# Fetching three 2 MB weight matrices in eighths between attention steps instead of whole ahead of them (hybrid decoder trunk, eight cores)

## The chip, the cores and the metric

The kernel runs on all 8 cores of one Trainium2 chip. Each core works on one prompt sequence of 2048 tokens and 16 single-token samples; the cores exchange nothing. The metric is the device time of the slowest core in microseconds. An execution is marked *slow* when one die (four cores) takes over 1% longer than the other at a lower granted TensorE clock, or when it is over 1.5% above the fastest of the same kernel; all others are *fast*, and slow runs are not compared with fast ones. Ratios below are the record's, of fast runs against fast runs of the same rounds, so they are not quite the ratio of the medians quoted.

## The reference

Two layers, each `x += mixer(norm(x)); x += memory_attention(norm(x)); x += mlp(norm(x))`, for a prompt group and a sample group that share all weights. What matters here is the attention of one layer and the MLP that follows it:

```python
def mem_attend(u, k, v, w_q, w_o):            # 4 heads of 256, 256 memory rows
    q = einsum('btd,de->bte', u, w_q)
    s = einsum('bthd,bnhd->bhtn', q, k) * (MEM_HEAD_DIM ** -0.5)
    p = softmax(s)
    return einsum('btd,de->bte', einsum('bhtn,bnhd->bthd', p, v), w_o)

def sq_relu_mlp(u, w_up, w_down):             # D_FF = 4096, done in four quarters
    h = relu(einsum('btd,df->btf', u, w_up))
    return einsum('btf,fd->btd', h * h, w_down)
```

Every sample has its own cached K and V (1 MB each in f32). Every prompt core has one K and V for its whole sequence, already multiplied into the weights.

## The kernel before

Weights live in five slots of SBUF, each one 1024 x 1024 matrix in bf16 (2 MB, for which 4 MB of f32 are read). `load` takes a free slot and starts one DMA from GpSimd (POOL), which casts f32 to bf16 on the way:

```python
def load(name, at=None):
    t = claim(name, at)
    dma(POOL, t(), DV(wsrc_sq(wsrc[name])), f"w{slot_of[name]}")
```

Just before the attention of a layer, the kernel loads the first quarter's up and down matrices and the second quarter's up matrix (`up0_0`, `dn0_0`, `up0_1`), each as soon as its slot is free. The MLP that needs them comes more than 100 us later.

During the attention, TensorE walks five tiles of the prompt. Twice per tile a *sample step* is put in between:

```python
def SDV(b):                                    # load V of sample b, in two halves
    v = VS[b % 2]
    for x in range(2):
        memset(v(x, sl(0, 4), sl(256, 257)), 1.0, eng=POOL)
        dma(POOL, v(x, sl(0, 4), sl(0, 256)), DV(cv_d[l, b, x*128:(x+1)*128, :]...), f"v{nm}{b % 2}")

def SA(b):                                     # scores of sample b on TensorE and DVE
    ...
    memset(PBZ[b % 2](), 0.0, eng=POOL)        # "the clear": empties the probability tile

def SE(b):                                     # ScalarE: probabilities into the tile
    act(PBZ[b % 2](sl(0, 8), b), SS(b % 4), AF.Exp, scale=1.0 / 16.0)

def sample(b):                                 # one sample step
    if b % N_ATT_S:
        SB(b - 1)                              # TensorE: PBZ times V, the "sample product"
    if b < last:
        SDK(b + 1); SDV(b + 1)
    SA(b)
```

`SE(b-1)` is called two chunks of matmuls before `sample(b)`; where nothing was late it started some 1.9 us before the sample product (249.68 and 251.55 us in the kernel before). GpSimd therefore runs, in this order and step after step: V half 0 of the next sample, V half 1, the clear. ScalarE's `SE` waits for the clear, and TensorE's sample product waits for `SE`.

A tracker derives every wait. Two of its lines matter:

```python
# Tracker.access: who must be waited for
if s.w is not None:
    deps.add(s.w)                              # the last writer of these bytes
if write:
    deps.update(s.rc.values())                 # and their readers
# Prog.add: how a DMA is waited for
if d.kind == "d":
    dw[d.chan] = self.chan_count[d.chan] * 16  # ALL DMAs issued so far on its semaphore
```

A DMA is waited for by the *current* count of its semaphore, not by its own. That is cautious for a good reason: the Trainium skill, "DMA: Bandwidth & Descriptors", section "Why a DMA increments its semaphore by 16 and not by 1", says that when two DMAs in flight share one semaphore, a lower count can be reached before the earlier one has fully landed.

The softmax here doesn't subtract the row's maximum and nothing guards it: scores larger than these inputs give would overflow.

## Time and profile before

| | before |
|---|---|
| median time, fast | 1732.6 us (1731.6 to 1734.0, 4 runs) |
| TensorE busy | 1599.2 us, 93% of the span |
| stall before the first sample product, layer 0 | 10.44 us |
| stall before the second sample product, layer 1 | 5.38 us |

From the page of the kernel before: the span, and TensorE's busy time, share and instructions.

```profile
span 1728.7 us, 28840 instructions; the slowest of 8 cores (1719.0 to 1728.7 us)
PE 1599.2 (93%) x9989; PEld 912.1 (53%) x10000; DVE 889.0 (51%) x1928; ACT 569.1 (33%) x1054; POOL 99.8 (6%) x218
```

TensorE is the bound. What can be won is its idle time. (PE is TensorE, PEld its weight loads, DVE VectorE, ACT ScalarE, POOL GpSimd. L350 is the helper through which every DMA is issued, L347 that of memsets, L315 that of ScalarE's activations; so instructions are told apart by their tiles.) The timeline of GpSimd around the start of layer 0's attention (start and duration in us; in brackets, the idle time before and what ended it):

```profile
161.19 1.08 POOL L350 DMA_DIRECT2D MEM<-w_up  x1 [30.86 <-PE PS L291]
183.09 0.87 POOL L350 DMA_DIRECT2D MEM<-w_down  x1 [20.82 <-PE PS L291]
186.64 0.87 POOL L350 DMA_DIRECT2D MEM<-w_up  x1 [2.68 <-PE PS L291]
...
187.58 0.75 POOL L350 DMA_DIRECT2D MEM<-cv  x1
...
222.97 0.74 POOL L350 DMA_DIRECT2D MEM<-cv  x1 [0.40 <-issue]
...
227.21 0.74 POOL L350 DMA_DIRECT2D MEM<-cv  x1 [3.37 <-DMA MEM<-cv]
```

Three matrices are issued just ahead of the first V load (`cv`), and the V load behind them took 33.4 us to land, by the chain of waits, where the median of all `cv` loads of that core is 5.0. The last two lines show something else: the second half of a V load goes out 4.24 us after the first, because GpSimd waits for the first to land, that is for its DMA to complete. That is the tracker's rule at work: the buffer was last written by an older DMA on the same semaphore, so half 1 waits for the count that includes half 0.

The timeline of TensorE, the two sample products (L295) that were late:

```profile
221.88 0.61 PE L295 MATMUL PS<-MEM 128*16 128x257 bf16 x8 [10.44 <-DMA MEM<-cv]
...
1126.54 0.61 PE L295 MATMUL PS<-MEM 128*16 128x257 bf16 x8 [5.38 <-ACT MEM L315]
```

The table of stretches (window, its length, busy time and instructions of five engines, granted clock, DMA share, GB/s) right after the first stall:

```profile
222.00:226.00 4.00, 4.00 (x18) 1.31 (x11) 2.30 (x11) 0.00 (x0) 0.98 (x3) 0.50 0.52 67
226.00:230.00 4.00, 3.77 (x16) 1.71 (x15) 1.04 (x6) 1.67 (x4) 0.95 (x2) 0.75 0.57 180
230.00:235.00 5.00, 5.00 (x39) 2.85 (x36) 3.66 (x7) 4.21 (x5) 0.00 (x0) 1.00 0.61 122
```

The granted clock is 0.50 for 4 us and 0.75 in the mean of the next 4, so it is halved for about 6 us after the stall. So a stall costs more than its idle time.

### The profile page before, as it was taken

The page shows a single profiled execution, that of the slowest core. Times are in us where ns is not written, and L with a number is a line of the kernel's source. Part 1 is how long each engine was busy: PE and PEld are TensorE (multiplying, and loading weights), DVE is VectorE, ACT ScalarE, POOL GpSimd, SP SyncE. Part 2 cuts the span into 40 slices and gives each one's busy share as a digit, 9 for nine tenths or more (in the row PEclk, how much of TensorE's full clock was granted, in tenths as well). Part 3 has the DMA queues.
Part 4 walks back from the last instruction along what each step waited for, and adds up shares of the span by engine and source line. Part 5 has one row for each costly group of instructions (what it writes and reads, how often), then busy time and mean ns, then how long its engine had stood idle before and what let it go on. Part 6 is the DMA issues. An engine that isn't in the chain of part 4 may idle for free.

```text
span 1728.7 us, 28840 instructions; the slowest of 8 cores (1719.0 to 1728.7 us)
## 1 busy us (share of the span) xinstructions
PE 1599.2 (93%) x9989; PEld 912.1 (53%) x10000; DVE 889.0 (51%) x1928; ACT 569.1 (33%) x1054; POOL 99.8 (6%) x218
## 2 busy tenths in 40 slices
PE   2657889999999999999999999999999999999985
PEld 2544445555565556555555555445555555555553
DVE  3544656646444444444666666666555444442357
ACT  2443633363212222223222223442552111113442
POOL 0200111011000000000000000110110000000000
PEclk9877989999999999999999999999999999999998
DMA  5959955354550740525300007954566353000112
GB/s 129 194 129 216 191 100 115 74 124 97 98 109 15 137 96 1 97 50 87 66 1 1 1 1 124 201 105 109 95 138 101 59 98 61 1 1 1 41 64 93
DMA packets 85495, 147.97 MB, mean 86 GB/s; under 512 B 3932, under 2 KB 37852, under 8 KB 85338
## 3 DMA queue, kind: packets, MB, share of 16 engines
q0 software_dynamic: 67552, 84.34, 31.6%
q1 hardware_dynamic: 17802, 61.80, 10.6%
q8 instruction: 83, 1.36, 0.3%
q14 instruction: 58, 0.48, 0.1%
HBM read 217.08 MB, written 14.36 MB: 134 GB/s over the span
## 4 chain that ended last, share of the span: by engine, by line
PE 83%; DMA 7%; DVE 5%; issue 2%; ACT 2%; SPq 0%; DVEq 0%; POOL 0%; ACTq 0%; POOLq 0%
PE PS L291 81%; DMA MEM<-cv 3%; DVE MEM L323 2%; DMA MEM<-x 2%; ACT MEM L315 2%; DVE MEM L344 2%; PE PS L295 1%; DMA MEM<-w_pool 1%; PE PS L300 1%; DMA MEM<-xs 0%; SPq L350 0%; DVE MEM L327 0%; DMA MEM<-mem 0%; DVE MEM L303 0%; ACT MEM L339 0%
## 5 line engine op out<-in xcount | busy, mean ns | idle before, releaser
L291 PE MATMUL PS<-MEM 128*128 128x416 bf16 (+6 forms) x9141 | 1530.9, 328 | 81.9 <-DVE MEM L323 64.9
L291 PEld LDWEIGHTS PS<-MEM 128*128 128x128 bf16 (+1 forms) x9152 | 849.9, 98 | 753.7 <-issue 134.7
L315 ACT ACTIVATE MEM<-PS 128x416 f32<-128x416 f32 (+6 forms) x510 | 260.2, 515 | 669.5 <-PE PS L291 605.7
L327 DVE TENSOR_TENSOR MEM<-PS,MEM 128x416 f32<-128x416 f32 (+5 forms) x525 | 295.7, 580 | 264.8 <-PE PS L291 256.0
L323 DVE SCALAR_TENSOR_TENSOR MEM<-MEM 128x416 bf16<-128x416 f32 (+8 forms) x346 | 200.3, 630 | 154.4 <-ACT MEM L315 126.4
L315 ACT ACTIVATE MEM<-MEM 128x416 bf16<-128x416 f32 (+13 forms) x317 | 204.9, 657 | 215.2 <-DVE MEM L327 106.3
L327 DVE TENSOR_TENSOR MEM<-MEM 128x416 bf16<-128x416 f32 (+4 forms) x284 | 161.8, 588 | 212.1 <-ACT MEM L315 183.8
L303 DVE SCALAR_TENSOR_TENSOR MEM<-MEM,PS 128x256 f32<-128x256 f32 x256 | 105.1, 420 | 81.0 <-PE PS L291 57.5
L339 ACT COPY MEM<-PS 128x512 f32<-128x512 f32 (+3 forms) x75 | 40.3, 538 | 118.4 <-PE PS L291 109.0
L344 DVE TENSOR_REDUCE MEM<-MEM 128x1 f32<-128x1024 f32 (+2 forms) x37 | 44.9, 1213 | 65.2 <-ACT MEM L315 65.1
L295 PE MATMUL PS<-MEM 128*16 128x257 bf16 (+2 forms) x640 | 52.0, 275 | 17.7 <-DMA MEM<-cv 10.4
L339 ACT CAST MEM<-PS 128x512 bf16<-128x512 f32 (+3 forms) x81 | 43.0, 558 | 70.4 <-PE PS L291 70.3
L295 PEld LDWEIGHTS PS<-MEM 128*16 128x16 bf16 (+2 forms) x640 | 40.2, 113 | 29.3 <-issue 28.8
L350 POOL DMA_DIRECT2D MEM<-cv x64 | 47.4, 741 | 118.8 <-DMA MEM<-cv 86.1
L315 ACT ACTIVATE PS<-PS 128x416 f32<-128x416 f32 (+3 forms) x68 | 33.4, 492 | 54.8 <-PE PS L291 54.4
L300 PE MATMUL PS<-MEM 128*128 128x128 f32 (+6 forms) x208 | 27.0, 282 | 17.6 <-DVE MEM L323 9.8
L323 DVE SCALAR_TENSOR_TENSOR MEM<-PS,MEM 128x512 f32<-128x512 f32 (+2 forms) x40 | 28.1, 743 | 15.2 <-ACT MEM L315 15.2
L300 PEld LDWEIGHTS PS<-MEM 128*128 128x128 f32 (+6 forms) x208 | 23.1, 142 | 21.2 <-issue 20.0
L347 POOL MEMSET MEM<- 128x4 bf16 (+1 forms) x96 | 14.9, 159 | 278.6 <-PE PS L295 220.8
L341 DVE CAST MEM<-PS 128x512 bf16<-128x512 f32 (+1 forms) x44 | 27.4, 640 | 5.2 <-PE PS L291 5.0
L303 DVE DVE_READ_ACCUMULATOR MEM<-MEM,PS 128x1 f32 x256 | 21.1, 82 | 0.0
L350 POOL DMA_DIRECT2D MEM<-w_down x8 | 7.0, 873 | 236.7 <-PE PS L291 224.5
(20 smaller groups left out, 78.0 us busy)
## 6 DMA issues: line engine op xcount, KB each, us to landing
MEM<-ck SPq DMA_DIRECT2D x64, 512.0 KB, 5.1
MEM<-w_up POOLq DMA_DIRECT2D x8, 2048.0 KB, 15.1
MEM<-w_down POOLq DMA_DIRECT2D x8, 2048.0 KB, 17.2
MEM<-cv POOLq DMA_DIRECT2D x64, 256.0 KB, 5.0
MEM<-x SPq DMA_DIRECT2D x16, 512.0 KB, 10.2
MEM<-w_o POOLq DMA_DIRECT2D x4, 2048.0 KB, 19.1
y<-MEM SPq DMA_DIRECT2D x15, 512.0 KB, 2.7
MEM<-w_conv_in POOLq DMA_DIRECT2D x3, 2048.0 KB, 13.4
```

Source lines behind the costliest of these rows:

```text
L291: P.add(PE, "c", lambda e, o=out.ap, l=lhsT.ap, r=rhs.ap: e.matmul(out=o, lhsT=l, rhs=r, start=start, stop=stop), [lhsT, rhs], [out])
L295: P.add(PE, "c", lambda e, o=out.ap, l=lhsT.ap, r=rhs.ap: e.matmul(out=o, lhsT=l, rhs=r, start=start, stop=stop, is_transpose=is_transpose ...
L300: P.add(PE, "c", lambda e, o=out.ap, i=in_.ap, d=ident.ap: e.transpose(out=o, in_=i, identity=d), [in_, ident], [out])
L303: P.add(DVE, "c", lambda e, o=out.ap, a=in0.ap, b=in1.ap, c=acc.ap: e.scalar_tensor_tensor(out=o, in0=a, scalar=1.0, in1=b, op0=ALU.mult, ...
L315: P.add(ACT, "c", lambda e, o=out.ap, i=in_.ap: e.activation(out=o, in_=i, func=func, bias=bias, scale=sc), rd, [out])
L323: P.add(eng, "c", lambda e, o=out.ap, a=in0.ap, b=in1.ap: e.scalar_tensor_tensor(out=o, in0=a, scalar=sc, in1=b, op0=op0, op1=op1), rd, [out])
L327: P.add(eng, "c", lambda e, o=out.ap, a=in0.ap, b=in1.ap: e.tensor_tensor(out=o, in0=a, in1=b, op=op), [in0, in1], [out])
L339: P.add(ACT, "c", lambda e, o=out.ap, i=in_.ap: e.copy(out=o, in_=i), [in_], [out])
L341: P.add(eng, "c", lambda e, o=out.ap, i=in_.ap: e.tensor_copy(out=o, in_=i), [in_], [out])
L344: P.add(eng, "c", lambda e, o=out.ap, i=in_.ap: e.tensor_reduce(out=o, in_=i, axis=AX.X, op=ALU.add), [in_], [out])
L347: P.add(eng, "c", lambda e, o=out.ap: e.memset(o, val), [], [out])
L350: return P.add(q, "d", lambda e, o=out.ap, i=in_.ap: e.dma_start(out=o, in_=i), [in_], [out], chan=chan, after=after)
```

## The change

The intent: keep the weights out of the way of the first V loads, and spread their bytes over attention tiles 1 to 3, since nobody needs them before the MLP. The diff, with the places of the calls cut to their core:

```diff
+    pieces = []
+    def load_slowly(name):
+        pieces.extend((name, kc) for kc in range(NCH))       # 8 pieces
+    def trickle():
+        if pieces:
+            name, kc = pieces.pop(0)
+            if kc == 0:
+                claim(name)
+            dma(POOL, W(name)(kc), DV(wsrc_sq(wsrc[name])[:, kc, :]), f"w{slot_of[name]}")
...
-        load(next(after))                # up0_0, dn0_0; likewise up{l}_1, up1_0, dn1_0
+        load_slowly(next(after))
...
             def mid_s(m, k=k):
+                if m % 2 and k:
+                    trickle()
...
-                O(k - 1, lambda ec: (pre() if ec == 1 else step() if ec == 3 else None))
+                O(k - 1, lambda ec: (trickle() if ec % 2 == 0 else pre() if ec == 1 else step() if ec == 3 else None))
...
-        assert not todo
+        assert not todo and not pieces
```

A piece is 128 rows of a matrix, 512 KB read and 256 KB written. Between two sample steps there are alternately three and five places for a piece. No matmul changes.

## The prediction

> **What bounds the kernel now.** TensorE: the page gives it 93% of the 1728.7 us span, and the chain of waits puts 83% on it. Idle TensorE at the ends (first 170 us, last 115 us) is untouched by this change. Two stalls are its target. The waits of layer 0's attention show TensorE idle for 10.4 us, to 221.9 us, for the first sample's V load: the timeline of GpSimd shows that load issued at 188, straight behind three whole weight matrices (161, 183, 187 us), and the chain gives the V load 33 us instead of the usual 4.5. In layer 1 a V load issued at 1104.9 lands at 1125 behind three matrices (1068 to 1086); TensorE idles 5.4 us. The Trainium skill, "TensorE: Matmul & The Clock Gate", Part 1, says an idle window of some 3.4 us halves the clock; here the granted clock is 0.89 to 0.93 around both stalls and 1.00 later, and the next sample interval takes 12.9 us instead of 10.5, so each stall costs some 2.4 us more. At stake: 10.4 + 5.4 + 2 x 2.4 = about 20 us (1.2%).
>
> **What the change does.** 3 matrices per layer become 24 pieces of 512 KB (read side), spread over attention tiles 1 to 3: no piece ahead of the first V loads, so both stalls should go. No matmul changes.
>
> **What it adds.** The kernel's dependency tracker makes a DMA that overwrites an older DMA's data wait for that channel's *current* count, including the pieces just issued. So each piece waits on GpSimd until the piece before it has landed. The trace shows this rule at work today: the second half of each V load starts 4.2 to 5.4 us after the first half (DMA wait 3.3 to 4.4 us), with a free queue. In layer 0 all three slots were last filled by a DMA, so all 24 pieces are serialized; in layer 1 two of three (the conv scratch slot was last written mostly by compute).
>
> GpSimd order per sample: V half 0, wait, V half 1, clear the small probability tile, then 3 or 5 pieces. Sample intervals on TensorE alternate 10.5 and 17.1 us (three and five pieces). Estimate, from V half 4.6 us, piece 4.0 to 4.2 us, issue 0.5 to 0.7: three pieces cost GpSimd 15 us, five cost 23; 38 per pair of samples against 27.6. The lag grows some 8 to 10 us per tile. Its victim: the clear of the probability tile comes after the second V issue, ScalarE's exponential waits for it, TensorE for that. By hand this gives layer 0 about 18 us of new stall including a re-throttle, layer 1 about 9.
>
> **Sum:** -20.7 + 18 + 10 = +7 us. Predicted 1740 us, range 1726 to 1764. Each 0.4 us on a piece moves it by about 8 to 10 us. Faster by over 2%: 0.01; within 2%: 0.92; slower by over 2%: 0.07.
>
> **What would show it.** Right: stalls at about 211 to 222 and 1121 us gone; GpSimd shows pieces spaced about 4 us with waits named DMA; V loads issued well after the sample product that frees their buffer; new TensorE idle of some 5 to 10 us twice in tiles 1 to 3 of layer 0, ended by ScalarE (behind GpSimd's memset), fewer in layer 1; clock dips there; GpSimd waiting on w_up/w_down DMAs for tens of us in total. MLP stages unchanged. Wrong: pieces issued back to back at 0.5 us (no serialization), then about 1713 us; or pieces landing in 3.4 us, then about 1727; or 5 us, about 1760.
>
> **What would make it wrong.** Piece landing time under eight cores' load; ScalarE order hiding more of the lag than I count; a slot order in layer 1 that serializes the third matrix too.

## The result, and the profile after

The change made the kernel slower: 1779.5 us median (1774.7 to 1781.7, 4 fast runs) against 1732.6, ratio 1.0266 with a 95% interval of 1.0244 to 1.0289. From the page of the kernel after:

```profile
span 1772.9 us, 28937 instructions; the slowest of 8 cores (1760.5 to 1772.9 us)
PE 1612.0 (91%) x10000; PEld 916.0 (52%) x10000; DVE 890.0 (50%) x1928; ACT 570.7 (32%) x1054; POOL 120.1 (7%) x260
```

The timeline of GpSimd in layer 0, part of tiles 1 and 2:

```profile
231.63 0.75 POOL L350 DMA_DIRECT2D MEM<-cv  x1
...
237.21 0.75 POOL L350 DMA_DIRECT2D MEM<-cv  x1 [4.70 <-DMA MEM<-cv]
...
238.09 0.55 POOL L350 DMA_DIRECT2D MEM<-w_up  x1
243.59 0.54 POOL L350 DMA_DIRECT2D MEM<-w_up  x1 [4.95 <-DMA MEM<-w_up]
244.12 0.54 POOL L350 DMA_DIRECT2D MEM<-w_down  x1
249.42 0.53 POOL L350 DMA_DIRECT2D MEM<-w_down  x1 [4.76 <-DMA MEM<-w_down]
254.38 0.53 POOL L350 DMA_DIRECT2D MEM<-w_down  x1 [4.43 <-DMA MEM<-w_down]
...
255.04 0.75 POOL L350 DMA_DIRECT2D MEM<-cv  x1
...
260.34 0.75 POOL L350 DMA_DIRECT2D MEM<-cv  x1 [4.43 <-DMA MEM<-cv]
261.08 0.22 POOL L347 MEMSET MEM<- 128x128 bf16 x1
```

Read it downward: each piece waits until the one before has landed (the bracket names the DMA), except at 244.12, where a new matrix starts in another slot with another semaphore. Only then come V (255.04 and 260.34) and the clear (261.08, L347). The timeline of ScalarE, then of TensorE, shows who waits for that clear:

```profile
261.39 0.24 ACT L315 ACTIVATE MEM<-MEM 128x8 bf16<-128x8 f32 x1 [10.03 <-POOL MEM L347]
```

```profile
208.65 0.40 PE L295 MATMUL PS<-MEM 128*16 128x257 bf16 x8
...
238.85 0.61 PE L295 MATMUL PS<-MEM 128*16 128x257 bf16 x8 [3.34 <-ACT MEM L315]
...
261.88 0.61 PE L295 MATMUL PS<-MEM 128*16 128x257 bf16 x8 [9.43 <-ACT MEM L315]
...
309.83 0.61 PE L295 MATMUL PS<-MEM 128*16 128x257 bf16 x8 [16.78 <-ACT MEM L315]
...
1144.73 0.40 PE L295 MATMUL PS<-MEM 128*16 128x257 bf16 x8
...
1197.68 0.61 PE L295 MATMUL PS<-MEM 128*16 128x257 bf16 x8 [15.21 <-ACT MEM L315]
...
1234.78 0.61 PE L295 MATMUL PS<-MEM 128*16 128x257 bf16 x8 [5.93 <-ACT MEM L315]
```

The stalls at the first sample product of layer 0 and at the second of layer 1 are gone (208.65 and 1144.73 have no bracket), as intended; five new ones, 3.3 to 16.8 us long, end with ScalarE (and two of 0.31 and 0.20 us, not shown). The waits by engine (total us, times, longest) of the kernel after; the kernel before has no wait on `w_up` or `w_down`, and a single one of 6.8 us of ScalarE for the memset:

```profile
POOL MEM L350 <- DMA MEM<-w_up: 81.1, 14, 8.2
...
ACT MEM L315 <- POOL MEM L347: 61.0, 9, 17.3
...
POOL MEM L350 <- DMA MEM<-w_down: 33.8, 6, 6.6
```

And the table of stretches after the stall that ends at 261.88:

```profile
262.00:266.00 4.00, 4.00 (x18) 1.29 (x11) 2.31 (x11) 0.00 (x0) 0.00 (x0) 0.50 0.92 131
266.00:270.00 4.00, 4.00 (x15) 1.81 (x14) 2.13 (x8) 0.00 (x0) 0.54 (x1) 0.61 0.57 152
270.00:276.00 6.00, 6.00 (x36) 3.33 (x35) 1.18 (x2) 1.04 (x2) 1.52 (x4) 1.00 0.45 117
```

**The account closes.** The time from the first to the eighth sample product, in a version without any stall (shown below), is 92.6 us in layer 0 and 94.6 us in layer 1. After the change it is 132.2 and 122.8 us: 39.6 + 28.2 = 67.8 us too long. In the kernel before it is 95.4 and 102.6 us, 2.8 + 8.0 too long, and the 10.44 us ahead of its first product come on top: 21.2 us. The difference is 67.8 - 21.2 = 46.6 us; the medians differ by 46.9. The rest of the kernel hardly changed: the spans of the two profiled executions differ by 44.2 us, because the one after came to its first sample product 2.8 us earlier (208.65 against 221.88 - 10.44). Of the 67.8 us, 51.2 are idle TensorE (the brackets); the other 16.6 are matmuls at half clock after the stalls, since the intervals that follow the five stalls are 3.1 to 3.5 us too long each.

### The profile page after: what moved, and what is told of

It is laid out like the page before. It is cut to its first block, busy times and chain, and to the rows that moved or that the text cites. A ratio compares the mean times of both kernels' runs of the same rounds, so it can differ in the third digit from the quotient of the medians.

```text
span 1772.9 us, 28937 instructions; the slowest of 8 cores (1760.5 to 1772.9 us)
## 1 busy us (share of the span) xinstructions
PE 1612.0 (91%) x10000; PEld 916.0 (52%) x10000; DVE 890.0 (50%) x1928; ACT 570.7 (32%) x1054; POOL 120.1 (7%) x260
## 4 chain that ended last, share of the span: by engine, by line
PE 76%; DMA 12%; DVE 4%; issue 4%; ACT 2%; SPq 0%; POOL 0%; DVEq 0%; ACTq 0%; POOLq 0%
PE PS L291 75%; DMA MEM<-w_up 3%; DMA MEM<-cv 3%; DMA MEM<-w_down 2%; DVE MEM L323 2%; DMA MEM<-x 2%; ACT MEM L315 2%; DVE MEM L344 2%; PE PS L295 1%; DMA MEM<-w_pool 1%; PE PS L300 1%; SPq L350 0%; DMA MEM<-xs 0%; DVE MEM L327 0%; DMA MEM<-mem 0%
## 5 line engine op out<-in xcount | busy, mean ns | idle before, releaser
L350 POOL DMA_DIRECT2D MEM<-cv x64 | 47.6, 744 | 122.0 <-DMA MEM<-cv 89.2
L300 PE MATMUL PS<-MEM 128*128 128x128 f32 (+6 forms) x208 | 27.0, 281 | 15.9 <-DVE MEM L323 9.7
L350 POOL DMA_DIRECT2D MEM<-w_up x36 | 20.7, 576 | 258.6 <-PE PS L291 177.5
L350 POOL DMA_DIRECT2D MEM<-w_down x22 | 13.9, 632 | 240.9 <-PE PS L291 194.4
L347 POOL MEMSET MEM<- 128x4 bf16 (+1 forms) x96 | 15.3, 162 | 193.8 <-PE PS L295 129.0
```

The source lines that it names most:

```text
L300: P.add(PE, "c", lambda e, o=out.ap, i=in_.ap, d=ident.ap: e.transpose(out=o, in_=i, identity=d), [in_, ident], [out])
L347: P.add(eng, "c", lambda e, o=out.ap: e.memset(o, val), [], [out])
L350: return P.add(q, "d", lambda e, o=out.ap, i=in_.ap: e.dma_start(out=o, in_=i), [in_], [out], chan=chan, after=after)
```

## The experiments

Theory A: GpSimd waits one after another for the landing of every piece, and the V load and the clear stand behind this chain. Rival B: it is the bytes of the weights, moved into the time of the K and V loads, that make those late, whoever waits for what. "Excess" is the time from the first to the eighth sample product, less 92.6 or 94.6 us, layer 0 + layer 1, on the core named by the profile.

| run | edit to | median us (state) | ratio to before | excess us |
|---|---|---|---|---|
| after | - | 1779.5 (fast) | 1.027 | 39.6 + 28.2 |
| e1_own_chan | after | 1729.9 (fast) | 0.998 | 9.8 + 12.2 |
| e6_whole_spread | after | 1712.9 (fast) | 0.989 | 3.4 + 1.3 |
| e2_before_reader_rule | before | 1729.7 (fast) | 0.999 | 2.1 + 8.4, and 11.8 ahead |
| e4_clear_first | after | 1770.0 (fast) | 1.021 | 37.0 + 23.1 |
| e3_after_reader_rule | after | 1749.2 (slow) | - | none |
| e5_quarters | after | 1790.9 (slow) | - | 36.4 + 15.9 |
| e8_little_k | after | 1782.0 (slow) | - | 24.6 + 21.8 |
| e9_little_v | after | 1783.6 (slow) | - | 24.0 + 14.6 |
| e3b_reader_rule | after | 1711.5 (fast) | 0.985 | 0 + 0 |
| e10_spread_rule | after | 1710.3 (fast) | 0.985 | 0 + 0 |
| e11_little_k_v | after | 1735.3 (fast) | 0.999 | 19.6 + 11.2 |
| e12_v_own | after | 1743.5 (fast) | 1.003 | 22.5 + 12.8 |

In the four slow runs the median clock of die 1 was about 0.95 (0.96 at most, in three executions below 0.90) in every execution, also of the kernel before (1760.8 us); in one of e3, die 0 was slowed too. For these I use the profile of the undisturbed die 0 cores, and typical medians of that die: before 1726 us, e3 1700, e5 1749, e8 1746, e9 1741. The change itself was not run on that chip; its die 0 medians elsewhere were 1763 to 1767.

### A semaphore per piece (e1_own_chan)

```diff
-            dma(POOL, W(name)(kc), DV(...), f"w{slot_of[name]}")
+            dma(POOL, W(name)(kc), DV(...), f"w{slot_of[name]}_{kc}")
```

> The 24 pieces, at the same places and of the same size, but each with its own DMA semaphore, so that a piece no longer waits for the one before it; V's own chain is left. Theory A (the chain of landing waits on GpSimd): pieces go out 0.5 us apart, GpSimd's waits on w_up and w_down fall from 115 us to near 0, the TensorE stalls of both layers go, and the time is 1708 to 1720 us, below the kernel before. Rival B (the weights' bytes among the V and K loads slow these, whoever waits): stalls of 10 us and more stay and the time stays above 1760 us.

The chain of pieces is gone, and most of the loss with it: from ratio 1.027 to 0.998, far below what B allows. But the time is level with the kernel before, 10 us above the range of A: stalls of 7.00 us in layer 0 and of 0.69 and 9.14 us in layer 1 stayed. The timeline of TensorE, two of them:

```profile
252.84 0.61 PE L295 MATMUL PS<-MEM 128*16 128x257 bf16 x8 [7.00 <-ACT MEM L315]
...
1161.86 0.61 PE L295 MATMUL PS<-MEM 128*16 128x257 bf16 x8 [9.14 <-ACT MEM L315]
```

The timeline of GpSimd shows what comes before the first of these:

```profile
233.79 1.07 POOL L350 DMA_DIRECT2D MEM<-w_up  x2
234.86 1.60 POOL L350 DMA_DIRECT2D MEM<-w_down  x3
...
236.46 0.75 POOL L350 DMA_DIRECT2D MEM<-cv  x1
...
251.30 0.75 POOL L350 DMA_DIRECT2D MEM<-cv  x1 [13.97 <-DMA MEM<-cv]
```

Five pieces now go out 0.53 us apart, just ahead of a V half, which needs 14.8 us to its successor's start instead of 4.2 to 6.2. So the bytes do delay V (B is right about that), but this hurts here only because half 1 and the clear wait for half 0, as e3b will show.

### Whole matrices, one per tile (e6_whole_spread)

```diff
-        pieces.extend((name, kc) for kc in range(NCH))
+        pieces.extend([(name, 0)] + [None] * (NCH - 1))
 ...
-            dma(POOL, W(name)(kc), DV(...), f"w{slot_of[name]}")      # one eighth
+            load(p[0])                                                # the whole, where p is not None
```

> The same deferral without the split: one whole matrix at the place where its first piece stood, one per attention tile. Theory A: a single DMA has nothing of its own to wait for, so no chain; the first V loads are free of weights as in the change; 1710 to 1725 us, with perhaps one V load held behind a matrix. Rival B (weights inside the attention steps hurt by their bytes, a 2 MB burst most): 1750 us or more.

1712.9 us, ratio 0.989 (0.986 to 0.992). The same deferral without the split has no chain and beats both kernels, if by less than 2%. Deferring the bytes is good; what cost was the splitting under this tracker.

### The tracker mended (e2, e3, e3b)

If the old contents of a buffer were read by an instruction that the new write waits for anyway, that reader had already waited for the old DMA. The wait on the old DMA is then superfluous, and with it the wait on everything else on that semaphore:

```diff
         for s in self.segs[i:j]:
-            if s.w is not None:
+            if s.w is not None and not (write and s.rc):
                 deps.add(s.w)
```

> The kernel before, with a tracker that leaves out the wait on an older write where a reader of that write is waited for anyway; V halves then no longer wait for each other. Theory A: layer 1's 5.4 us stall (probability clear behind a V half behind three matrices) mostly goes, layer 0's 10.4 us (the V data itself late) stays: 1723 to 1730 us. Rival B: no change, 1731 to 1734 us.

On the kernel before it changed nothing: 1729.7 against 1730.3 us in the same rounds. My reading of layer 1's stall was too narrow. With the clear out of the way, the same sample product waits 6.42 us, now with the V data itself as the releaser (`DMA MEM<-cv`). Both were late behind the three matrices; the profile names only the later one.

> The change with the tracker that leaves out a wait on an older write where its reader is waited for: neither pieces nor V halves wait for each other. With separate semaphores for the pieces alone, 9.4 us of stall stayed in layer 0 and as much in layer 1, each behind a V half that took 12 to 15 us to land behind three to five pieces issued at once, with the other half and the clear of the probability tile waiting for it. If that rest is V's own chain (theory A again): the clear comes early, both stalls go, 1706 to 1718 us. If it is the V data itself late behind the pieces' bytes (theory B for the rest): 1725 to 1731 us, and the stall ends with a DMA from cv.

All runs of e3 fell in the slow state; its die 0 showed 1700 us against 1726 and, on the core looked at, no stall. (The 9.4 us of the expectation fits layer 0 of e1 only with the slow clock counted in: 7.00 us of idle, 9.8 of excess.) It was repeated:

> The change with the reader rule in the tracker, again, because all runs of the first try fell in the slow state of one die; its undisturbed die showed a median of 1700 us against 1726 for the kernel before, and no stall at all in either attention. Expected in the fast state: 1704 to 1711 us.

1711.5 us (one of its four runs was slow), half a microsecond above what was expected, ratio 0.985 (0.983 to 0.987). The first sample products of layer 0 in the timeline of TensorE of e3b, none with a bracket (nor has one of the first eight in layer 1):

```profile
211.22 0.40 PE L295 MATMUL PS<-MEM 128*16 128x257 bf16 x8
...
221.29 0.40 PE L295 MATMUL PS<-MEM 128*16 128x257 bf16 x8
...
238.00 0.40 PE L295 MATMUL PS<-MEM 128*16 128x257 bf16 x8
...
248.50 0.40 PE L295 MATMUL PS<-MEM 128*16 128x257 bf16 x8
...
265.65 0.40 PE L295 MATMUL PS<-MEM 128*16 128x257 bf16 x8
```

In its waits by engine GpSimd waits for no DMA of `w_up`, `w_down` or `cv`, and ScalarE not for the memset. So the same pieces, of the same bytes, at the same places in the program, cost nothing once no one waits for their landing. Nor is it the work of issuing them: GpSimd runs 260 instructions here as in the change (117.3 us busy against 120.1). Rival B falls as the cause of the loss: delay of the V data alone never reaches TensorE here.

### The mended tracker with whole matrices (e10_spread_rule)

The edits of e6 and e3 together.

> The whole matrices, one per attention tile, together with the reader rule. The whole matrices alone kept stalls of 1.7 and 1.3 us, ended by ScalarE behind the clear that waits for a V half. Expected: these go too and the time is that of the pieces with the rule, 1704 to 1711 us; then the split into eighths earns nothing by itself. If the split is worth something: 3 us or more above the pieces with the rule.

1710.3 us against 1711.5 for the pieces, ratios 0.985 and 0.985. The split into eighths earns nothing by itself that these runs could tell; one matrix per tile is enough.

### The clear ahead of the V load (e4_clear_first)

```diff
             if b % N_ATT_S:
                 SB(b - 1)
+            memset(PBZ[b % 2](), 0.0, eng=POOL)
             if b < last:
                 SDK(b + 1); SDV(b + 1)
```

(and the memset is taken out of `SA`.)

> The change, with the clear of the probability tile put ahead of the next V load in GpSimd's order, still behind the pieces. Theory A with the victim named in the prediction: the clear comes one V half (4.6 to 5.5 us) earlier per chain, so each layer loses about 5 us of stall once: 1765 to 1772 us, and the stalls still end with ScalarE behind GpSimd. If instead the late V data were the victim: no change, 1779 us.

1770.0 us, inside what was expected, and the stalls still end with ScalarE. The excess fell by 5.1 us in layer 1, the time of a V half, but only by 2.6 us in layer 0: the clear still stands behind the pieces, and the chain is as long as before.

### Half of the chain taken away (e12_v_own)

```diff
-                dma(POOL, v(...), DV(...), f"v{nm}{b % 2}")
+                dma(POOL, v(...), DV(...), f"v{nm}{b % 2}_{x}")
```

> The change with its chained pieces, but each half of V on a semaphore of its own, so that the second half no longer waits for the first. The V half takes 5.9 us out of a chain of some 46 us per pair of samples (2 x 5.9 of V, 6 x 5.9 of pieces), so the chain is still longer than TensorE's 27.6 us: 34 to 36 us. Expected: the stalls of either layer shrink by about half, 1735 to 1755 us, between the change (1779) and both chains gone (about 1708).

1743.5 us, as expected: with the V halves out of the chain and the pieces still in it, about half of the excess remains (35.3 of 67.8 us). Together with e1 this divides the chain into its two links; neither alone is enough.

### Fewer and larger pieces (e5_quarters)

```diff
-        pieces.extend((name, kc) for kc in range(NCH))
+        pieces.extend((name, kc) for kc in range(0, NCH, 2))
 ...
-            dma(POOL, W(name)(kc), DV(...[:, kc, :]), ...)
+            dma(POOL, W(name)(sl(kc, kc + 2)), DV(...[:, kc:kc + 2, :]), ...)
```

> The change with 12 pieces of 1 MB instead of 24 of 512 KB, in the first 12 of the 24 places, still chained. Theory A: what counts is the number of waits in a chain between two V loads, 6 or 7 of them per layer instead of 13, each of 7 to 9 us instead of 6: the stalls of layer 0 fall from about 30 us to 10 or 20, the whole to 1740 to 1765 us. Rival B (bytes among the V loads, here packed twice as densely in half the time): 1779 us or more.

All runs were slow, so the time cannot be held against the expectation. On a die 0 core the excess is 52.3 us instead of 67.8: the direction fits A, the size less well. A piece of 1 MB took 8.7 us in the mean, and the stalls came early: 6.25 and 23.44 us in layer 0, the longer one behind a group of five pieces. Together they are above the 10 to 20 us that I expected.

### Why a piece takes six microseconds (e8, e9, e11)

These three shrink the K or V loads beside the pieces and so compute wrong sample rows (relative errors of 0.08 to 0.11 in the two sample outputs). The table counts the time from a piece's issue to the next one's, where GpSimd stood idle before the next.

```diff
+                w = 64 if 0 < b < N_ATT_S else D                       # e8, in SDK
-                dma(SP, KS[i](), DV(ck_d[l, b, x*128:(x+1)*128, :]), ...)
+                dma(SP, KS[i](sl(0, w)), DV(ck_d[l, b, x*128:(x+1)*128, 0:w]), ...)
+                w = 32 if 1 < b < N_ATT_S else 256                     # e9, in SDV; e11 has both
```

> The change, with wrong results for the sample rows on purpose: the K loads of samples 1 to 7 of each layer are cut to 64 of 1024 columns. It asks why a piece takes 5.9 to 6.6 us and not the 4.0 to 4.2 predicted. If the K loads beside it are why: pieces fall to about 4.2 to 4.6 us at the median and the time to 1735 to 1755 us, near what was predicted. If a piece costs that by itself, or through the V half in its own queue: 5.5 us or more and 1770 us or more.

> The change, with wrong results for the sample rows on purpose: the V loads of samples 2 to 7 of each layer are cut to 32 of 256 columns per head, the number of loads and waits unchanged. If the V half just ahead of a piece in the same queue is why the pieces take long: those right behind a V half fall from about 7 to 4.5 us, the median of all to about 5, and the time to 1750 to 1765 us (the V halves themselves also land about 1 us sooner). If it is K or the pieces alone: median 5.5 us or more, time above 1765 us.

> The change with K and V loads of the first half of the samples both cut (wrong sample rows on purpose); chain and number of loads unchanged. Cut one at a time, pieces went from 6.1 us in the mean to 5.3 in both cases. If K and V traffic are the whole excess over the 4.0 to 4.2 us of the prediction: 4.2 to 4.5 us, and a time of 1715 to 1735 us. If a piece is slow by itself: 5 us or more.

| | mean us per piece (median) | pieces counted |
|---|---|---|
| after | 6.1 (5.9), 4.3 to 9.6 | 195, all cores |
| little K | 5.3 (5.2) | 90, die 0 |
| little V | 5.3 (5.3) | 92, die 0 |
| little of both | 4.95 (4.8) | 179, all cores |

K or V traffic alone accounts for 0.6 to 0.8 us of a piece (5.95 us is the mean of the change's own die 0 cores), and both together for 1.1 us of an excess of about 2 over my estimate. So all three results lie between the two outcomes that I had written down: K, V and something else each have a share. (The times of e8 and e9 are of slow runs and decide nothing.) The last 0.8 us or so belongs to neither: left nearly alone, a piece takes as long as a V half took in the kernel before (4.75 us median over all cores). What makes it so was not pursued; other cores' traffic on the same memory is a candidate that no run isolates. With both cut, the kernel took 1735.3 us, with an excess of 30.8 us; the prediction had 28. That these agree is in part luck: a V half, cut, took 4.5 us in the mean, as assumed (4.6), but a piece took 4.95 and not 4.0 to 4.2, and by the prediction's own sensitivity that should have given some 45 us.

## Why the prediction was wrong

- **What bounds the kernel, and the 20 us at stake: right.** The stalls before, with their slow clock, sum to 21.2 us, predicted 20.7; versions without stalls run at 1710 to 1712 us, ratio 0.985 to the kernel before, which is some 26 us and so a little more than the stalls of the one core profiled.
- **The chain of landing waits on GpSimd, that its lag grows from tile to tile, its victim (the clear, ScalarE's exponential, TensorE): right.** The waits named DMA, the brackets ending with ScalarE, e1, e3b and e12 show each part.
- **The failed step is the term "piece 4.0 to 4.2 us", and with it "V half 4.6 us".** Measured: 6.1 us per piece and 6.5 us per V half in the mean (5.9 each at the median). I had taken V halves of a quiet stretch on one core, and the low end of those (4.2 us), granting the pieces a discount for their shorter issue (0.53 against 0.74 us). I did not ask what the pieces would do to the loads beside them and these to the pieces. "38 per pair of samples against 27.6" was in fact 2 x 5.9 + 6 x 5.9 = 47 us at the medians (layer 0 of the core profiled: 45.4 us from the V load at 209.66 to the one at 255.04, then 47.6), so the lag grew by 18 to 20 us per tile and not by 8 to 10. My own sensitivity ("each 0.4 us on a piece moves it by 8 to 10 us") turns 2 us on a piece into 40 to 50; the miss was 39. That this fits so well is partly luck too: from e11 to the change the excess grew by 37 us for 1.1 us on a piece and 2 on a V half.
- **The cost of a stall's slow clock: under-sized.** Predicted 2.4 us per stall, read off two intervals of the kernel before. The intervals after the five stalls are 3.1 to 3.5 us too long, and there were five.
- **"new stall 18 us including a re-throttle" in layer 0, 9 or 10 in layer 1** rests on these: 39.6 and 28.2 us were measured.
- **The range** reached to 1764, and gave "slower by over 2%" a chance of 0.07, although I had written down that 5 us per piece would mean 1760. A range on a sum that multiplies guessed durations by 36 waits per core (24 of pieces and 12 of V halves) should have been as wide as that duration's doubt.

## What to carry to other kernels

Before splitting a transfer, look at what its buffer's reuse rule makes the *issuing engine* wait for: on an engine that runs its instructions in order, as GpSimd did in every timeline here, a chain of landings holds up everything that comes behind it, and it is the short instruction at the end of the queue, here a 0.2 us memset, that stalls the matmuls. Move bytes out of the way by deferring them whole first, and split only if that leaves something to win; here it left nothing that could be measured. When a plan multiplies one duration many times, take it from a stretch as loaded as the plan will make it, and let its spread set the range.

## What the Trainium skill lacked or had wrong

- "DMA: Bandwidth & Descriptors", "Anatomy of one DMA — SWDGE (gpsimd) path", fits a DMA from GpSimd as about 2.0 us plus bytes over 436 GB/s, which for the 512 KB that a piece reads is an estimate of 3.2 us. Chained one behind another in this kernel on eight cores, a piece takes 4.95 us in the mean nearly alone and 6.1 us beside the K and V loads, from issue to issue. The page's bandwidth figures go as far as both cores of an HBM pair streaming; it has none for one such DMA beside the mixed loads of eight cores.
- The same section says that waits happen on the issuing sequencer while the DMA engines only drain their queues. The traces agree: in the change GpSimd itself stood idle 4.95 us before the piece at 243.59, until a DMA had landed. What it leaves out is the price of the queue: a V half issued behind five pieces (e1) needed 14.8 us to its successor's start instead of 4.2 to 6.2.
- "Why a DMA increments its semaphore by 16 and not by 1" asks for one semaphore per in-flight slot. No page warns of the converse, that a cautious wait on a shared semaphore's full count turns pieces into a chain of landings: ratio 1.027 to the kernel before against 0.998 with a semaphore per piece, some 49 us here.
- "TensorE: Matmul & The Clock Gate", "Part 1: The HAM clock gate (the "warmup" mystery)", says that after an idle window of some 3.4 us the clock is halved until about 3.4 us of sustained work. The granted clock agrees with the two values, 0.50 and 1.00, but the way back took about twice as long here: after the stall that ends at 261.88 the clock is 0.50 for the first 4 us and 0.61 over the next 4, which puts the return at 7.2 us, and after the other four of the change the same working gives 6.4 to 7.1 us; some 3.1 to 3.5 us were lost per stall. The page also says that the window runs freely, which could explain a part of this; no run here tests it. And one stall of only 1.69 us (e6, layer 0, to 249.24) was followed by a clock of 0.50 too (251 to 253 us).
